# Transposing the FFN input rows once per pair of tiles, before their seven combinations are formed

## The chip, the cores and the metric

The kernel runs on one core of a Trainium2 chip. The core has five engines with instruction queues of their own: PE (TensorE, matmuls and transposes, results in PSUM), DVE (VectorE), ACT (ScalarE), POOL (GpSimd) and SP (SyncE, here only a queue that issues transfers). POOL issues transfers too. The metric is the device time of one execution in microseconds.

## What is computed

One layer of a streaming encoder, in float32, for 2048 prompt rows and 128 sample rows of width 1024: a mixer (attention over a band of chunks beside a convolution), attention into 256 memory tokens, and a SwiGLU feed-forward layer of width 2816. What matters here is the last part of the reference:

```python
h = rmsnorm(x, g_mem_pre)
x = x + rmsnorm(memory_attention(h, mk, mv, w_mq, w_mo), g_mem_post)
h = rmsnorm(x, g_ffn_pre)
f = (jax.nn.silu(h @ w_gate) * (h @ w_up)) @ w_down
x = x + rmsnorm(f, g_ffn_post)
```

## The kernel before

**Stages.** The stages follow one another: memory keys, input projection, attention, mixer output, cross attention (`phase_cross`), gate and up (`gate_up`), down (`down`). The tile framework orders the instructions of each engine ahead of time by a model of their durations, with program order as priority; each engine then runs its queue in that order and waits on semaphores where a producer isn't ready.

**Arithmetic.** A float32 matrix product is made of three products of a rounded half and a rest: each operand is split into `hi` (a cast on ACT) and `lo` (value minus `hi`, mostly on DVE), and PE computes hi x hi, hi x lo and lo x hi (`mm3`, L281 to L283, and `mm3h`, L289).

**Cross stage.** It goes over 16 prompt tiles of 128 rows. For tile t the program has `probs(t)` (eight transposes of the softmax result, L1281, split by L1284 and L1285), `scores(t+1)` (48 matmuls, then the softmax), `norm(t+2)` (load of x1, square and multiply, eight transposes at L316, split) and `values(t)` (48 matmuls, then `postnorm`: square, multiply at L337, the residual added on POOL at L338, store of x2 at L339). The transposes of `probs` and `norm` use one PSUM buffer, tag "t". The load of `norm` needs an "xt" buffer that an earlier `postnorm` has finished with. The sample tile (number 16) is handled earlier, beside other work.

**Fast multiplication of the FFN.** Gate and up are computed with seven block products in place of eight (a Strassen scheme): one half of the blocks is the two 512-wide halves of the input rows of two tiles, the other is weight blocks. So the two tiles of a pair, xa and xb, give seven combinations of their halves. There are three groups of three pairs (`PAIRS`; the last pair is the two halves of the sample tile, 64 rows each), and group g is processed for all 22 hidden chunks of 128 before the next one.

**`natural(g, p)`** (L1298) makes the combinations for one pair: for each tile it loads x2 (L1306, SP), squares it (L1309, ACT), makes the reciprocal root (L1311, L1312, POOL) and multiplies by it and the gain (L1313, DVE). Then POOL forms the four differences (L1314, L1316, L1318, L1320) and stores the seven blocks in rows by 512 columns to `hn[g]` in DRAM, four stores (L1315, L1317, L1319, L1321). Its three buffers "na", "nb" and "nt" exist once. It is called in the cross stage after tile t, from t = 4 on, for the first pair whose tiles are both earlier than t; the pair that remains is called in the first chunks of gate and up (L1484).

**`tform(g, j)`** (L1382) brings combination j of a group into SBUF as `hi` and `lo` with the model dimension on partitions, as PE needs it. For each of the three pairs: load 512 columns of the rows from `hn` (L1388, SP, three buffers "nat"), four transposes (L1391) into a PSUM buffer (two, tag "tr"), cast out of PSUM (L1393, ACT), subtraction out of PSUM (L1394, DVE). A group has 7 x 3 = 21 such blocks. The calls stand: for group 0 before the first chunk, with raised priority, and for each next group during the last chunk of the group before it, form j right after product j has released its buffer (`after(j)`). These two stretches are called turns.

**A chunk** (one f) has seven products of 12 matmuls; the first ends with a copy out of PSUM on ACT (L1450). Beside it run `wforms` for the next chunk (two loads, four POOL operations L1408 to L1411, seven casts L1413, seven subtractions L1414), the activation on DVE (L1469, L1476, L1478 from SBUF, the others from PSUM), and after each second chunk four POOL operations (`act_forms`, L1503 to L1506).

## Time and profile before

| What | Value |
|---|---|
| median of 3 runs | 3066.88 us (3065.92 to 3074.45) |
| span of the profiled execution | 3068.5 us (its own total is not given) |
| mean granted clock of PE | 0.980 |
| cross stage, tiles 0 to 15 | about 1281 to 1644 us of the span |
| gate and up | about 1644 to 2600 us |
| transposes of `tform` (L1391) | 252, in 63 sets of four |
| products of a chunk, groups 0 and 1 | 14.56 us per chunk in steady work |
| products of a chunk, group 2 (320 columns) | 12.32 us per chunk |

In the rows of the profile, a group of instructions is named by its line, engine and operation, with output and input tiles, shape and count; then the busy time in microseconds, the mean duration of one in ns, and the idle time of the engine just before it with what ended it. A mean duration of a matmul is its latency; back to back they overlap, so what one costs PE is read from the distance of the starts, or from the chain of work that ended last. Tiles in SBUF are named sbf, sbr, sbx and flexb, PSUM is psb.

### The profile page before, as it was taken

The numbers are of one execution on the slowest core, as the hardware profiler recorded it, in microseconds if no ns is written. First come the engines' busy times: TensorE is split into PE (matmuls) and PEld (weight loads), VectorE is DVE, ScalarE is ACT, GpSimd is POOL, SyncE is SP. The second block draws the span as 40 slices with busy tenths as digits, with TensorE's granted clock in tenths as the row PEclk, the third lists the DMA queues.
The fourth block names the chain that finished last, engine by engine and source line by source line (L and its number), as shares of the span: only waits on it lengthen the run. The fifth ranks groups of instructions, "written<-read, shape, count | busy, mean of one in ns | idle before, by whom it ended". The sixth has DMA issues, their size and how long they took to land.

```text
span 3068.5 us, 46049 instructions
## 1 busy us (share of the span) xinstructions
PE 2958.1 (96%) x16924; PEld 2725.9 (89%) x16924; DVE 2135.7 (70%) x3077; ACT 1358.3 (44%) x2718; POOL 1419.9 (46%) x1336
## 2 busy tenths in 40 slices
PE   8999999968999999999999999999999999999998
PEld 8999999957888788788888999999999999888786
DVE  6696886746668456635456888877878999556565
ACT  4544455546767344423234333443334444433432
POOL 0267595621112324325355655555555776524413
PEclk9999999978999999999999999999999999999999
DMA  8635252645663456423246333454425345756664
GB/s 302 246 111 176 90 172 97 189 150 135 155 158 141 147 205 209 168 69 124 91 157 206 132 135 135 149 176 159 154 105 174 144 144 178 261 186 210 217 202 161
DMA packets 217693, 500.17 MB, mean 163 GB/s; under 512 B 40757, under 2 KB 104765, under 8 KB 208627
## 3 DMA queue, kind: packets, MB, share of 16 engines
q1 hardware_dynamic: 181035, 427.53, 41.6%
q0 software_dynamic: 36432, 69.70, 7.3%
q8 instruction: 133, 2.18, 0.3%
q14 instruction: 93, 0.76, 0.1%
HBM read 365.97 MB, written 141.81 MB: 165 GB/s over the span
## 4 chain that ended last, share of the span: by engine, by line
PE 38%; DMA 4%; DVE 3%; issue 2%; POOL 2%; ACT 1%; SPq 0%; DVEq 0%; POOLq 0%; ACTq 0%
PE psb L283 12%; PE psb L282 12%; PE psb L281 12%; DMA sbf<-in_w_down_dram 2%; PE psb L289 1%; POOL sbf L1536 1%; DMA sbf<-x 1%; PE psb L1391 1%; DMA sbf<-hn 0%; DVE sbr L1597 0%; DVE sbr L1540 0%; DVE sbr L1414 0%; POOL sbf L338 0%; DMA sbf<-in_w_gate_dram 0%; DVE flexb L1476 0%
## 5 line engine op out<-in xcount | busy, mean ns | idle before, releaser
L281 PE MATMUL psb<-sbr 128*128 128x384 f32 (+3 forms) x2808 | 945.6, 338 | 11.1 <-DVE sbf L688 7.1
L282 PE MATMUL psb<-sbr 128*128 128x384 f32 (+3 forms) x2356 | 808.5, 343 | 2.6 <-DVE sbr L318 2.4
L283 PE MATMUL psb<-sbr 128*128 128x512 f32 (+3 forms) x1848 | 633.4, 344 | 2.7 <-DVE sbr L1597 2.5
L281 PEld LDWEIGHTS psb<-sbr 128*128 128x128 f32 x2808 | 533.0, 190 | 41.0 <-DVE sbf L688 7.3
L283 PE MATMUL psb<-sbr,sbx 128*128 128x384 f32 (+2 forms) x1484 | 478.5, 323 | 0.0
L282 PEld LDWEIGHTS psb<-sbr 128*128 128x128 f32 x2356 | 448.1, 190 | 29.3 <-DVE sbr L318 2.7
L283 PEld LDWEIGHTS psb<-sbr 128*128 128x128 f32 x1848 | 348.6, 189 | 31.6 <-DVE sbr L1597 4.9
L289 PE MATMUL psb<-sbr 128*128 128x512 f32 x1200 | 295.5, 394 | 3.0 <-DVE flexb L1044 1.7
L1414 DVE TENSOR_TENSOR sbr<-sbf,sbr 128x512 fp32r<-128x512 f32 x258 | 263.5, 1024 | 40.7 <-ACT sbr L1413 40.0
L1413 ACT CAST sbr<-sbf 128x512 fp32r<-128x512 f32 x258 | 159.3, 620 | 280.5 <-PE psb L282 232.3
L283 PEld LDWEIGHTS psb<-sbr,sbx 128*128 128x128 f32 x1484 | 282.7, 191 | 0.1
L522 DVE SCALAR_TENSOR_TENSOR psb<-sbf,psb 128x768 f32<-128x768 f32 (+1 forms) x290 | 264.5, 912 | 6.2
L289 PEld LDWEIGHTS psb<-sbr 128*128 128x128 f32 x1200 | 222.4, 189 | 48.7 <-DVE flexb L1044 2.1
L1597 DVE TENSOR_TENSOR sbr<-sbf,sbr 128x384 fp32r<-128x384 f32 (+1 forms) x231 | 168.4, 752 | 93.7 <-ACT sbr L1596 91.2
L276 POOL TENSOR_TENSOR sbx<-sbf,sbr 128x1024 fp32r<-128x1024 f32 x60 | 150.9, 2517 | 85.8 <-ACT sbr L275 81.2
L1596 ACT CAST sbr<-sbf 128x384 fp32r<-128x384 f32 (+1 forms) x231 | 110.7, 497 | 167.7 <-PE psb L282 150.1
L1536 POOL TENSOR_TENSOR sbf<-sbf 128x512 f32<-128x512 f32 x77 | 105.7, 1377 | 168.3 <-DMA sbf<-in_w_down_dram 166.7
L532 POOL TENSOR_TENSOR flexb<-flexb,flexb 128x128 f32<-128x128 f32 (+1 forms) x180 | 168.5, 936 | 30.9 <-ACT flexb L531 20.3
L281 PE MATMUL psb<-sbr,sbx 128*128 128x384 f32 (+1 forms) x524 | 170.6, 327 | 1.2 <-ACT sbr L1393 0.7
L1413 ACT CAST sbx<-sbf 128x512 fp32r<-128x512 f32 x153 | 94.7, 621 | 161.6 <-PE psb L282 152.7
L1414 DVE TENSOR_TENSOR sbx<-sbf,sbx 128x512 fp32r<-128x512 f32 x153 | 151.5, 992 | 15.7 <-ACT sbx L1413 15.5
L1408 POOL TENSOR_TENSOR sbf<-sbf 128x512 f32<-128x512 f32 x66 | 98.6, 1493 | 107.6 <-DVE sbr L1414 50.8
(339 smaller groups left out, 6294.0 us busy)
## 6 DMA issues: line engine op xcount, KB each, us to landing
af<-flexb SPq DMA_DIRECT2D x33, 1344.0 KB, 5.6
sbf<-in_w_down_dram SPq DMA_DIRECT2D x154, 256.0 KB, 3.9
sbf<-af SPq DMA_DIRECT2D x90, 384.0 KB, 4.0
sbf<-in_w_gate_dram SPq DMA_DIRECT2D x66, 512.0 KB, 3.3
sbf<-in_w_up_dram SPq DMA_DIRECT2D x66, 512.0 KB, 3.5
sbf<-x SPq DMA_DIRECT2D x49, 512.0 KB, 3.9
sbf<-in_w_in_dram SPq DMA_DIRECT2D x48, 512.0 KB, 4.2
sbr<-ks POOLq DMA_DIRECT2D x16, 1024.0 KB, 33.9
```

The lines of the kernel that those rows point to most:

```text
L276: self.lo_engine.tensor_tensor(lo[:, :], wf[:, :], hi[:, :].bitcast(F32), ALU.subtract)
L281: nc.tensor.matmul(ps, lh, rh, start=start, stop=False, **kw)
L282: nc.tensor.matmul(ps, lh, rl, start=False, stop=False, **kw)
L283: nc.tensor.matmul(ps, ll, rh, start=False, stop=stop, **kw)
L289: nc.tensor.matmul(y[o], l, r[:, o * 512:(o + 1) * 512], start=start and x == 0, stop=stop and x == 2)
L522: nc.vector.scalar_tensor_tensor(acc if w < CW - 1 else o, src(w), cwt[:, j, w:w + 1], acc, ALU.mult, ALU.add)
L532: nc.gpsimd.tensor_tensor(o, o, v, ALU.add)
L1413: nc.scalar.copy(hs[j][:, :], src[j])
L1414: nc.vector.tensor_tensor(ls[j][:, :], src[j], hs[j][:, :].bitcast(F32), ALU.subtract)
L1536: nc.gpsimd.tensor_tensor(acc[:, :], acc[:, :], q[:, :], ALU.add if s > 0 else ALU.subtract)
L1596: nc.scalar.copy(ch[:, m], a[:, x, m])
L1597: nc.vector.tensor_tensor(cl[:, m], a[:, x, m], ch[:, m].bitcast(F32), ALU.subtract)
```

## The change

`hn[g]` becomes [form, pair position, partition, columns]: the blocks are kept transposed, 128 of the model dimension on partitions and 4 x n columns (four blocks of n rows; n is 128, for the sample pair 64).

`natural` becomes a generator. Each tile is loaded into the buffer "nt" (now `c`), normalised there, transposed in two sets of four on PE, and copied by ACT into "na" or "nb". The four differences are formed by POOL from the transposed tiles, with "nt" taking two of them, and stored. The generator stops after the normalisation of each tile, so that it is advanced at three places. In the cross stage: right after `values(t)` (load and normalisation of the first tile), before the fifth of the eight steps of the next `scores` (transposes of the first tile, load and normalisation of the second), and before the seventh step of the next `values` (transposes of the second, differences and stores). It is started only for t below 14, so two pairs, (2,0) and (2,1), remain for gate and up, where one of its parts is run after each of the first chunks, with the PSUM buffers "tr". In the cross stage it uses the PSUM buffer "t".

`tform` loads a block and splits it straight from SBUF: no transposes, no PSUM. The subtraction for the third pair goes to POOL.

```diff
-        self.hn = [self.dram(f"hn{g}", [P, 3, 7, 512]) for g in range(3)]
+        self.hn = [self.dram(f"hn{g}", [3, 7, P, 512]) for g in range(3)]
...
+            for k in range(KC):
+                if k == 4:
+                    next(side, None)
                 self.mm3h(halves(s), hh[:, k, :], hl[:, k, :], f1[k][0], f1[k][1], k == 0, k == KC - 1)
...
+                if k == 6:
+                    next(side, None)
                 self.mm3h(halves(y), ph[:, k, :], pl[:, k, :], f2[k][0], f2[k][1], k == 0, k == KC - 1)
...
-        def natural(g, p):
+        def natural(g, p, ps, tag):
             n = PAIRS[g][p][2]
+            xa, xb, c = [self.t(pool, [P, D], F32, tg) for tg in ("na", "nb", "nt")]
             for x, (t, r0) in zip((xa, xb), PAIRS[g][p][:2]):
+                nc.sync.dma_start(c[:n, :], self.x2[t][r0:r0 + n, :])
...
+                nc.vector.scalar_tensor_tensor(c[:n, :], c[:n, :], r[:n, :], gffn[:n, :], ALU.mult, ALU.mult)
+                yield True
+                for k0 in range(0, KC, 4):
+                    if k0 == 0 or tag == "tr":
+                        pt = self.t(ps, [P, KC if tag == "t" else 4, P], F32, tag)
+                    kb = k0 if tag == "t" else 0
+                    for k in range(4):
+                        nc.tensor.transpose(pt[:, kb + k, :n], c[:n, (k0 + k) * P:(k0 + k + 1) * P],
+                                            self.ident[:n, :n])
+                    v = x[:, k0 * n:(k0 + 4) * n].rearrange("p (k q) -> p k q", q=n)
+                    nc.scalar.copy(v, pt[:, kb:kb + 4, :n])
+            dst = self.hn[g][p]
+            h0, h1 = slice(0, 4 * n), slice(4 * n, 8 * n)
+            def put(first, src, count=2):
+                nc.gpsimd.dma_start(dst[first:first + count, :, :4 * n].rearrange("f p c -> p f c"),
+                                    src.rearrange("p (f c) -> p f c", f=count))
+            both = slice(0, 8 * n)
+            nc.gpsimd.tensor_tensor(c[:, h0], xb[:, h0], xa[:, h0], ALU.subtract)
+            put(0, xa[:, both])
+            nc.gpsimd.tensor_tensor(c[:, h1], xb[:, h1], c[:, h0], ALU.subtract)
+            put(4, c[:, both])
+            nc.gpsimd.tensor_tensor(xb[:, h0], xb[:, h1], xb[:, h0], ALU.subtract)
+            put(2, xb[:, both])
+            nc.gpsimd.tensor_tensor(xa[:, h1], c[:, h1], xa[:, h1], ALU.subtract)
+            put(6, xa[:, h1], 1)
...
-                if ready and t >= 4:
-                    natural(g, p)
+                if ready and 4 <= t < NPT - 2:
+                    side = natural(g, p, ps_t, "t")
+                    next(side)
...
-                nc.sync.dma_start(x[:n, :], self.hn[g][:n, p, TFORM[j], :])
-                ps = self.t(ps_tr, [P, 4, P], F32, "tr")
-                for k in range(4):
-                    nc.tensor.transpose(ps[:, k, :n], x[:n, k * P:(k + 1) * P], self.ident[:n, :n])
+                nc.sync.dma_start(x[:, :4 * n], self.hn[g][p, TFORM[j], :, :4 * n])
+                x = x[:, :4 * n].rearrange("p (k q) -> p k q", q=n)
                 c = slice(p * P, p * P + n)
-                nc.scalar.copy(hi[:, :, c], ps[:, :, :n])
-                nc.vector.tensor_tensor(lo[:, :, c], ps[:, :, :n], hi[:, :, c].bitcast(F32), ALU.subtract)
+                nc.scalar.copy(hi[:, :, c], x)
+                engine = nc.gpsimd if p == 2 else nc.vector
+                engine.tensor_tensor(lo[:, :, c], x, hi[:, :, c].bitcast(F32), ALU.subtract)
...
-                    if g == 0 and x == 1 and self.todo:
-                        self.natural(*self.todo.pop(0))
+                    if g == 0:
+                        if next(side, None) is None and self.todo:
+                            side = self.natural(*self.todo.pop(0), ps_tr, "tr")
+                            next(side)
```

More of the change, by code (lines that the diff above doesn't have):

```diff
@@ L1258, in norm @@
             return xt, hh, hl
+        side = iter(())
         def scores(hh, hl, where="s"):
@@ L1296, in phase_cross @@
         gffn = self.gain(Region().at("gffn", 4, (self.gffn, [0])), "g_ffn_pre", "gffn")
[L1298 removed]
+        def natural(g, p, ps, tag):
             n = PAIRS[g][p][2]
[L1300 to L1303 removed]
+            xa, xb, c = [self.t(pool, [P, D], F32, tg) for tg in ("na", "nb", "nt")]
             for x, (t, r0) in zip((xa, xb), PAIRS[g][p][:2]):
[L1305 to L1306 removed]
+                nc.sync.dma_start(c[:n, :], self.x2[t][r0:r0 + n, :])
                 junk = self.t(pool, [P, D], BF16, "junk", 1)
                 ss = self.t(pool, [P, 1], F32, "ss", 6)
[L1309 removed]
+                nc.scalar.activation(junk[:n, :], c[:n, :], AF.Square, accum_out=ss[:n, :])
                 r = self.t(pool, [P, 1], F32, "rstd", 6)
@@ L1422, in product @@
                          skip_group_check=True)
+        side = iter(())
         with self.tc.high_priority(offset=HP):
```

16 lines of the change are left out of this document (removed).

## The prediction

> **What bounds the kernel now.** I read the page first (totals, chain), then the stretches around the two stages that the change touches, then single rows.
>
> ```profile
> span 3068.5 us, 46049 instructions
> PE 2958.1 (96%) x16924; PEld 2725.9 (89%) x16924; DVE 2135.7 (70%) x3077; ACT 1358.3 (44%) x2718; POOL 1419.9 (46%) x1336
> PE 38%; DMA 4%; DVE 3%; issue 2%; POOL 2%; ACT 1%; SPq 0%; DVEq 0%; POOLq 0%; ACTq 0%
> ```
>
> TensorE (PE) is busy 96% of the span and is by far the largest owner of the chain. So an instruction taken from PE is time won, unless PE was waiting where it stood anyway. Busy time by stretch (columns: length; then PE, weight loads, DVE, ACT, POOL busy with counts; granted clock; DMA) shows where it waits:
>
> ```profile
> 1380.00:1405.00 25.00, 25.00 (x120) 20.85 (x120) 10.45 (x13) 8.32 (x18) 9.25 (x13) 1.00 0.19 68
> 1645.00:1690.00 45.00, 39.93 (x225) 36.82 (x224) 36.65 (x45) 23.30 (x45) 33.71 (x32) 0.92 0.73 251
> 2003.00:2032.00 29.00, 26.52 (x165) 25.50 (x165) 19.20 (x32) 11.68 (x21) 7.89 (x7) 1.00 0.54 181
> ```
>
> The cross stage (first row) is full, and its other engines are half idle: there PE alone sets the pace. The start of the gate-and-up stage (second row) loses 5.1 us of 45, runs at a clock of 0.92, and DVE and POOL are nearly as busy as PE. The turn from token group 0 to 1 (third row) loses 2.5 us.
>
> **What the transposes cost on PE.** The chain, in order of time, gives a set of four (L1391) and one of eight (L1281) between back-to-back matmuls; the group row gives the count and the waits in front:
>
> ```profile
> 2000.70 0.44 PE psb L1391 x4
> 1608.16 0.87 PE psb L1281 x8
> L1391 PE MATMUL psb<-ident,sbf 128*128 128x128 f32 (+1 forms) x252 | 37.5, 270 | 5.2 <-DMA sbf<-hn 3.3 <-DVE sbr L1394 1.8
> ```
>
> Removed: 63 sets of four, 63 x 0.44 = 27.7 us. Added: 18 tiles of eight. The new rule (t below 14, both tiles earlier than t) starts pairs after t = 4, 5, 6, 7, 10, 11, 12, so 14 tiles lie in the cross stage, 14 x 0.87 = 12.2 us, all of it paid since PE is full there. The other four (pairs (2,0) and (2,1)) go into the first hidden chunks of gate-and-up, 8 sets x 0.44 = 3.5 us. Net on PE 27.7 - 15.7 = 12 us less. But where the 27.7 us stood decides. The copy of the first product out of PSUM (L1450) runs once for each of the 22 hidden chunks of a group and dates them:
>
> ```profile
> 1648.21 0.48 ACT L1450 COPY sbf<-psb 128x384 f32<-128x384 f32 x1
> 1737.35 0.47 ACT L1450 COPY sbf<-psb 128x384 f32<-128x384 f32 x1
> 1955.75 0.48 ACT L1450 COPY sbf<-psb 128x384 f32<-128x384 f32 x1
> 1970.31 0.47 ACT L1450 COPY sbf<-psb 128x384 f32<-128x384 f32 x1
> 2070.82 0.47 ACT L1450 COPY sbf<-psb 128x384 f32<-128x384 f32 x1
> 2303.78 0.47 ACT L1450 COPY sbf<-psb 128x384 f32<-128x384 f32 x1
> 2390.72 0.42 ACT L1450 COPY sbf<-psb 128x320 f32<-128x320 f32 x1
> 2403.04 0.42 ACT L1450 COPY sbf<-psb 128x320 f32<-128x320 f32 x1
> ```
>
> A steady chunk takes 1970.31 - 1955.75 = 14.56 us, in group 2 (320 columns) 2403.04 - 2390.72 = 12.32. *Start*: five chunks take 89.1, 16.3 more than 5 x 14.56; 15 sets of transposes are 6.6 of it, the rest is waits and slow clock. *Turn 1*: six chunks take 100.5, 13.1 over; 21 sets are 9.2, the rest waits. *Turn 2*: 86.9 against 14.56 + 5 x 12.32 = 76.2, 10.8 over, nearly all transposes. The six sets ahead of 1648 stand in the full tail of the cross stage: 2.6 us, gone for certain. The slow clock is seen in the spacing of matmuls, 0.32 us at the start against 0.17 later:
>
> ```profile
> 1655.79 0.52 PE L283 MATMUL psb<-sbr 128*128 128x384 f32 x1
> 1656.11 0.52 PE L281 MATMUL psb<-sbr 128*128 128x384 f32 x1
> ...
> 1999.67 0.33 PE L281 MATMUL psb<-sbr 128*128 128x384 f32 x1
> 1999.84 0.33 PE L282 MATMUL psb<-sbr 128*128 128x384 f32 x1
> ```
>
> **What takes over where the transposes go.** The subtraction that makes the low half (L1394) read PSUM; now it reads SBUF, as L1414 does, 42 times on DVE and 21 times (third pair) on POOL. The source rows give ns min/median/max, the timeline shows DVE, then POOL, in steady work:
>
> ```profile
> L1394 DVE TENSOR_TENSOR sbr<-psb,sbr x45: 408/681/693, 1633.0 to 2339.1; 128x512 fp32r<-128x512 f32 x40, 128x256 fp32r<-128x256 f32 x5
> L1414 DVE TENSOR_TENSOR sbr<-sbf,sbr x258: 674/693/1983, 1612.2 to 2584.5; 128x512 fp32r<-128x512 f32 x129
> ```
> ```profile
> 2473.97 1.39 DVE L1414 TENSOR_TENSOR sbr<-sbf,sbr 128x512 fp32r<-128x512 f32 x1
> ...
> 2475.67 1.39 DVE L1414 TENSOR_TENSOR sbr<-sbf,sbr 128x512 fp32r<-128x512 f32 x1
> ```
> ```profile
> 2473.18 1.63 POOL L1409 TENSOR_TENSOR sbf<-sbf 128x512 f32<-128x512 f32 x1
> 2474.77 1.75 POOL L1410 TENSOR_TENSOR sbf<-sbf 128x512 f32<-128x512 f32 x1
> ```
>
> The PSUM reader never exceeds 693 ns; the SBUF reader ends only when POOL's operation has ended, and one of each takes 2475.67 - 2473.97 = 1.70 us together. I split this into 0.5 for DVE and 1.2 for POOL (an estimate). A chunk then needs 7 + 3 such DVE operations (the three on 384 columns, by their width, at 0.38) and 4 + 2 of POOL (the activations' forms, on 384 columns too, at 0.9): 3.5 + 1.1 + 4.8 + 1.8 = 11.2 us of this shared resource. A turn adds 14 x 0.5 + 7 x 1.2 = 15.4. Six chunks with a turn need 6 x 11.2 + 15.4 = 82.6 us. Against PE's own 87.4 at turn 1 this fits. At turn 2 PE would need 76.2, so 82.6 becomes the floor, 4.3 under today's 86.9, unless the forms prepared ahead and later chunks take up part. At the start 5 x 11.2 + 15.4, and two pairs at 2 x 1.1 + 4 x 1.2 = 7 each, make 85.4 against 89.1. (Pair (2,0) leaves the end of the cross stage: its two loads go on SP behind the 21 form loads and the next weight loads, its squares, multiplies, combinations and stores come some 20 us later, still within these five chunks, so the move itself counts nothing; if it fell behind them it would cost the 7 us in steady chunks, where 11.2 of 14.56 leaves 3.4 each.) The Trainium skill has this as a rule (GPSIMD Engine Reference, section 8, Key points): GpSimd shares its SBUF interfaces with VectorE, with contention for DVE instructions that have two SBUF inputs. The trace agrees: 1.39 us beside POOL, 0.69 alone. By that rule turn 2 gains some 4 us, without it 9; it is the second rival below.
>
> So I take: start -4, the 3.5 us of new transposes included (ends 0 and -13), turn 1 -11 (ends -4 and -13: PE is the floor, but part of the 2.5 us wait for loads stays, since each load buffer is now held until the subtraction instead of the transpose), turn 2 -5 (ends -4 and -11, nearer to the shared floor).
>
> **What the cross stage pays beside the 12.2 us.** Per natural: the x2 load, square, two small POOL operations and the DVE multiply are as before; new are four ACT copies (0.56 each by L1393), and the four POOL combinations now wait for them. ACT has room (8.3 of 25). The three paired stores become two runs of 2 KB per partition where one of 4 KB stood; no row shows such an issue on POOL; between nothing and another 0.62 each it hides in POOL's idle time (9.3 of 25 busy); uncovered, it is 18 x 0.62 = 11 us at most.
> ```profile
> L1393 ACT CAST sbr<-psb 128x512 fp32r<-128x512 f32 (+1 forms) x54 | 29.8, 563 | 28.3 <-PE psb L1391 26.9 <-DVE sbr L1394 1.3
> ...
> L1315 POOL DMA_DIRECT2D hn<-sbf x9 | 5.6, 618 | 1.6 <-DVE sbf L1313 1.5
> ```
>
> What waits now, and what is queued behind it: PE for the normalised tile, with the matmuls of scores and values behind; SP's load of the second tile until PE has read the first out of the same buffer, with norm's x1 load behind; POOL's combinations for ACT's copies, with postnorm's add and store behind, whose end frees the buffer for that x1 load. PE already pays for such chains in this stage:
>
> ```profile
> PE psb L316 <- DVE sbf L313: 4.0, 5, 1.6
> ...
> PE psb L316 <- DVE sbr L318: 3.3, 1, 3.3
> ```
>
> Five waits when norm's multiply comes late, 0.8 us on average, 1.6 at most. For 14 new sets the bounds are 0 and 14 x 1.6 = 22; I take a wait of 0.8 at one set in four, 2.8 us.
>
> **Sum**: 12.2 + 2.8 - 2.6 - 4 - 11 - 5 = -7.6 us. All of it is from one execution with a span of 3068.5; its total is not shown, and its span lies 1.6 above the median 3066.88 of the runs. I apply the difference to the median: **3059 us**.
>
> **Rivals.** *All of it is won*: PE's own work is the floor at the start and both turns, and cross gets no new waits: 12.2 - 2.6 - 12.8 (16.3 less 3.5) - 13.1 - 10.8 = -27; with 6 us of waits left, -21, so 3046. For it: DVE and POOL have idle gaps at turn 1 (19.2 and 7.9 busy of 29). Against: the start.
>
> *The subtraction on the shared interface takes the transposes' place*: nothing at the start, 5 at turn 1, 4 at turn 2: 12.2 + 2.8 - 2.6 - 9 = +3.4, so 3070. This is also the case in which the change doesn't do what it says: the PE work goes, the time doesn't.
>
> *Slower: the loop through the one buffer in the cross stage.* Tile one and tile two are both normalised in "nt", which then takes combinations and is stored before the next pair may load:
>
> ```profile
> DMA to landing us min/median/max: 3.1/4.1/4.5
> ...
> L1309 ACT ACTIVATE sbf<-sbf 128x1024 bf16<-128x1024 f32 x16 | 16.9, 1058 | 16.1 <-DMA sbf<-x 16.0
> L1312 POOL TENSOR_TENSOR sbf<-sbf,mhalf 128x1 f32<-128x1 f32 x16 | 8.9, 558 | 0.9
> L1313 DVE SCALAR_TENSOR_TENSOR sbf<-sbf,flexb 128x1024 f32<-128x1024 f32 x16 | 30.8, 1924 | 24.7 <-POOL sbf L1312 24.6
> L1314 POOL TENSOR_TENSOR sbf<-sbf 128x512 f32<-128x512 f32 x8 | 10.6, 1330 | 0.8 <-DVE sbf L1313 0.8
> L1316 POOL TENSOR_TENSOR sbf<-sbf 128x512 f32<-128x512 f32 x8 | 15.9, 1982 | 0.6
> ...
> DMA to landing us min/median/max: 3.3/3.7/4.8
> ```
> ```profile
> 1390.68 1.04 PE L1281 MATMUL psb<-ident,sbf 128*128 128x128 f32 x8
> ...
> 1414.24 1.04 PE L1281 MATMUL psb<-ident,sbf 128*128 128x128 f32 x8
> ```
>
> A tile takes 4.1 + 1.2 + 1.1 + 1.9 + 0.9 = 9.2; two tiles, copies 1.2, two combinations with issues 4.5 and the store 3.7 make 27.8 us. An iteration of cross is 1414.24 - 1390.68 = 23.6, with the new transposes 25.3. Pairs that follow each other (three steps after t = 4, two after t = 10) slip 2.5 us each. PE can run the next scores meanwhile, half of (23.6 - 1.7) = 11 us, against three slips of 7.5: so I hold it hidden. It decides when the loop passes 25.3 + 11/3 = 29 us. If PE pays the five slips (12.5) and 0.8 at all 14 sets (11.2 instead of 2.8): -7.6 + 12.5 + 8.4 = +13, 3080.
>
> **Chances.** Within 0.3% (9.2 us) a measurement of this kernel can't be told from no change. Forecast 0.46 (own range 3053 to 3066; 0.17 of it below 3057.7), all won 0.25, shared interface 0.17 (0.03 of it above 3076.1), loop 0.12. So faster 0.17 + 0.25 = 0.42, slower 0.12 + 0.03 = 0.15, same 0.43. The range 3043 to 3077 leaves out the better end of the second case and most of the loop.
>
> **What would show it.** Right: 14 sets of eight in the cross stage and about 15 us more there; six chunks at turn 1 near 90 us; at turn 2 near 82; the new subtraction with a maximum far above 693 ns. Wrong: waits of PE for the DVE multiply in the cross stage adding to over 10 us (loop), turns at 77 and 88 us (all won), or turns as long as before with PE waiting for the subtraction.

## The result: slower by 3%, two thirds of it in the cross stage

The changed kernel takes 3166.57 us in the median of four runs, the kernel before 3070.66, also of four: a ratio of 1.0305, with a 95% interval of 1.0285 to 1.0325. The prediction was 3059 us with a range up to 3077, so it was wrong in its direction and far outside its range. Line numbers move in the new program: `probs` has its transposes at L1285 and its split at L1288 and L1289, `natural` its load at L1310, square at L1313, multiply at L1317, transposes at L1324, copies on ACT at L1327, stores at L1332; `tform` has its load at L1411, cast at L1414 and subtraction at L1416; the copy of the first product is L1473, the weights' subtraction L1436. In both programs L317 and L318 are the split (cast, subtraction) of `norm`'s tile behind its transposes at L316. The kernels of the experiments have line numbers of their own.

The page of the changed kernel, its totals:

```profile
span 3171.6 us, 45871 instructions
PE 2984.3 (94%) x16816; PEld 2742.5 (86%) x16816; DVE 2114.7 (67%) x3056; ACT 1378.0 (43%) x2754; POOL 1458.5 (46%) x1357
```

PE has fewer instructions than before (16816 against 16924) and is busy for longer (2984.3 against 2958.1 us): it ran slower, and it also waited more. The view by stretches, cut at the same events in both kernels, says where. The columns are start and end, length, busy time (and count) of PE, weight loads, DVE, ACT and POOL, granted clock, DMA. The rows are: the cross stage from its first `probs` to its last; from there to the first chunk; the start (five chunks); turn 1; turn 2. First before, then after:

```profile
1281.65:1628.40 346.75, 341.54 (x1617) 283.35 (x1616) 161.89 (x174) 111.89 (x243) 142.03 (x170) 1.00 0.32 112
1628.40:1648.21 19.81, 19.37 (x106) 16.26 (x104) 7.51 (x10) 8.42 (x15) 5.72 (x9) 1.00 0.48 154
1648.21:1737.35 89.14, 83.39 (x471) 80.37 (x472) 79.37 (x98) 37.56 (x73) 67.21 (x55) 0.96 0.56 201
1970.31:2070.82 100.51, 98.03 (x594) 96.40 (x593) 82.16 (x118) 44.10 (x82) 49.76 (x37) 1.00 0.55 191
2303.78:2390.72 86.94, 86.23 (x583) 83.47 (x582) 75.44 (x117) 42.12 (x83) 49.17 (x42) 1.00 0.46 161
```

```profile
1288.05:1703.99 415.94, 370.74 (x1726) 306.12 (x1725) 142.11 (x176) 128.28 (x274) 142.87 (x170) 0.93 0.28 94
1703.99:1727.22 23.23, 19.23 (x92) 15.82 (x90) 9.71 (x10) 9.93 (x17) 9.38 (x9) 1.00 0.46 149
1727.22:1821.05 93.83, 81.17 (x432) 79.33 (x433) 78.35 (x88) 40.20 (x77) 64.97 (x52) 0.89 0.44 153
2060.86:2166.68 105.82, 95.69 (x506) 93.30 (x505) 88.23 (x110) 44.94 (x82) 62.39 (x45) 0.94 0.52 179
2399.64:2486.99 87.35, 78.82 (x507) 76.18 (x506) 82.64 (x113) 41.49 (x83) 61.07 (x51) 1.00 0.52 175
```

The cross stage is 69.2 us longer. PE's idle time there rose from 5.2 to 45.2 us, and its busy time by 29.2, of which the new transposes (the group L1324) are 17.5; the granted clock fell from 1.00 to 0.93. The three stretches of gate and up lost their transposes (PE's instructions fell from 594 to 506 at turn 1) and gained nothing: +4.7, +5.3, +0.4. Turn 2 shows it most plainly: PE is busy 7.4 us less and the stretch is as long as before. Beside these rows, the sixteen chunks between start and turn 1 take 239.8 us (1821.05 to 2060.86) instead of 233.0, and the lead into the first chunk 3.4 more. That makes 89.8 of the 103.1 us between the two spans (the medians differ by 95.9; the profiled execution of the changed kernel is the slowest of its four). The other 13 lie ahead of the cross stage (6.4) and behind the last chunk (6.8), where the two programs do the same work; a second profile of the kernel before, below, moved by 3.5 and 3.7 us at the same places, and e6 says why these 13 are not put down to the change.

**What PE waits for in the cross stage.** The view of waits of the changed kernel over that stretch (who waited, for whom; total, times, longest):

```profile
PE psb L316 <- DVE sbf L313: 33.4, 5, 9.0
PE psb L289 <- ACT sbr L317: 8.1, 7, 1.3
PE psb L1324 <- DVE sbr L318: 2.5, 2, 1.3
```

The first row was 4.0 us before. It isn't `natural` that PE waits for, but `norm`: the transposes at L316 stand in PE's queue, and the multiply at L313 in front of them is late. There were five such waits, and five pairs in the stage follow directly on another pair. The timeline of one such iteration of the changed kernel shows how, PE first (start, duration, engine, line; in brackets the idle time before and its releaser):

```profile
1430.29 1.03 PE L1285 MATMUL psb<-ident,sbf 128*128 128x128 f32 x8
...
1444.57 1.03 PE L1324 MATMUL psb<-ident,sbf 128*128 128x128 f32 x8
1445.36 3.43 PE L289 MATMUL psb<-flexb,sbr 128*128 128x512 f32 x14
1454.57 1.94 PE L316 MATMUL psb<-ident,sbf 128*128 128x128 f32 x8 [5.78 <-DVE sbf L313]
1457.62 2.07 PE L289 MATMUL psb<-sbr 128*128 128x512 f32 x4 [1.10 <-ACT sbr L317]
1459.49 1.91 PE L1324 MATMUL psb<-ident,sbf 128*128 128x128 f32 x8
```

and the other queues of the same iteration:

```profile
1434.41 11.55 SPq L1310 DMA_DIRECT2D sbf<-x  x2
```
```profile
1439.20 1.06 ACT L1313 ACTIVATE sbf<-sbf 128x1024 bf16<-128x1024 f32 x1 [6.82 <-DMA sbf<-x]
...
1449.04 1.06 ACT L1313 ACTIVATE sbf<-sbf 128x1024 bf16<-128x1024 f32 x1 [2.75 <-DMA sbf<-x]
...
1450.21 1.06 ACT L306 ACTIVATE sbf<-sbf 128x1024 bf16<-128x1024 f32 x1
```
```profile
1453.14 1.28 DVE L313 SCALAR_TENSOR_TENSOR sbf<-sbf 128x1024 f32<-128x1024 f32 x1 [0.72 <-POOL sbf L299]
```

Read upwards from the wait: L313 needs `norm`'s square (L306 at 1450.21), whose load had been issued at 1426.28; the three loads that SP issued in these 25 us landed in 3.3 us in the median. But ACT runs its queue in order, and ahead of that square stands the square of the pair's second tile (L1313 at 1449.04), which waits for a load. That load may start only when PE has read the first tile out of the one buffer (L1324 at 1444.57). And the first tile itself was loaded late, since the buffer had still to be stored for the pair before (the load at 1434.41, with the square waiting 6.82 us for it). So a loop through one buffer reaches, by ACT's queue, a chain that has nothing to do with it.

### The profile page after: what moved, and what is told of

It is laid out like the page before. It is cut to its first block, busy times and chain, and to the rows that moved or that the text cites. A ratio compares the mean times of both kernels' runs of the same rounds, so it can differ in the third digit from the quotient of the medians.

```text
span 3171.6 us, 45871 instructions
## 1 busy us (share of the span) xinstructions
PE 2984.3 (94%) x16816; PEld 2742.5 (86%) x16816; DVE 2114.7 (67%) x3056; ACT 1378.0 (43%) x2754; POOL 1458.5 (46%) x1357
## 5 line engine op out<-in xcount | busy, mean ns | idle before, releaser
L289 PE MATMUL psb<-sbr 128*128 128x512 f32 x1200 | 307.4, 404 | 13.0 <-ACT sbr L317 8.1
L1436 DVE TENSOR_TENSOR sbr<-sbf,sbr 128x512 fp32r<-128x512 f32 x258 | 256.3, 999 | 28.8 <-ACT sbr L1435 24.6
L1561 POOL TENSOR_TENSOR sbf<-sbf 128x512 f32<-128x512 f32 x77 | 107.1, 1397 | 171.6 <-DMA sbf<-in_w_down_dram 169.9
L1436 DVE TENSOR_TENSOR sbx<-sbf,sbx 128x512 fp32r<-128x512 f32 x153 | 143.6, 943 | 6.1 <-ACT sbx L1435 5.4
L275 ACT CAST sbr<-sbf 128x1024 fp32r<-128x1024 f32 x98 | 102.4, 1049 | 101.2 <-PE psb L282 51.5
```

The lines of the kernel that those rows point to most:

```text
L289: nc.tensor.matmul(y[o], l, r[:, o * 512:(o + 1) * 512], start=start and x == 0, stop=stop and x == 2)
L1436: nc.vector.tensor_tensor(ls[j][:, :], src[j], hs[j][:, :].bitcast(F32), ALU.subtract)
L1561: nc.gpsimd.tensor_tensor(acc[:, :], acc[:, :], q[:, :], ALU.add if s > 0 else ALU.subtract)
```

## The experiments

The table sets the stage lengths of all profiles side by side, cut as above. "Half" means the gate-and-up half of the change alone.

| Kernel | cross | start | turn 1 | turn 2 | ratio to before, 95% |
|---|---|---|---|---|---|
| before, first profile | 346.8 | 89.1 | 100.5 | 86.9 | |
| before, second profile | 346.7 | 90.1 | 99.7 | 87.0 | 0.9999 [0.9973, 1.0024] |
| changed | 415.9 | 93.8 | 105.8 | 87.3 | 1.0305 [1.0285, 1.0325] |
| e0 transposes only | 354.0 | 89.8 | 100.4 | 87.0 | 1.0046 [1.0030, 1.0063] |
| e1 cross half alone | 419.0 | 94.3 | 101.2 | 87.3 | 1.0280 [1.0264, 1.0295] |
| e2 half | 353.9 | 99.8 | 102.0 | 88.6 | 1.0092 [1.0076, 1.0108] |
| e7 half, subtraction on DVE alone | 353.6 | 91.4 | 97.6 | 89.0 | 1.0082 [1.0059, 1.0105] |
| e10 half, rows of 4 KB | 347.2 | 93.2 | 101.6 | 88.6 | 1.0047 [1.0029, 1.0065] |
| e9 half, subtraction out of PSUM | 352.3 | 89.6 | 93.7 | 81.3 | 0.9981 [0.9968, 0.9994] |
| e14 half, both | 348.2 | 86.6 | 93.1 | 80.5 | 0.9972 [0.9956, 0.9988] |
| e3 pairs apart | 369.8 | 89.9 | 107.4 | 87.9 | 1.0143 [1.0109, 1.0176] |
| e4 own buffer | 372.6 | 88.4 | 105.4 | 88.3 | 1.0103 [1.0064, 1.0142] |
| e5 both of these | 365.3 | 91.2 | 107.8 | 90.1 | 1.0148 [1.0111, 1.0184] |
| e12 square after norm | 389.1 | 91.2 | 106.1 | 88.2 | 1.0190 [1.0175, 1.0206] |
| e11 mended | 371.8 | 79.9 | 94.9 | 80.8 | 1.0024 [1.0004, 1.0044] |
| e13 mended, start after norm | 365.3 | 85.7 | 93.3 | 80.3 | 1.0000 [0.9986, 1.0015] |

### Which half, and is it the transposes?

**e0: the transposes alone.** The kernel before, plus

```diff
+        def extra():
+            if now[0] in (5, 6, 7, 8, 11, 12, 13):
+                pt = self.t(ps_t, [P, KC, P], F32, "t")
+                for k in range(KC):
+                    nc.tensor.transpose(pt[:, k, :], gpost[:, k * P:(k + 1) * P], self.ident[:, :])
...
+                if k == 4:
+                    extra()
...
+                if k == 6:
+                    extra()
```

> The kernel before, with 14 extra sets of eight transposes (of a constant tile, read by nothing) at the places in the cross stage where the changed kernel has its own: in the scores and in the values of seven iterations, out through the same PSUM place. Theory A (the cross stage loses its 69 us in waits on the chain that feeds those transposes): only the transposes are paid, 14 x 0.87 = 12 us, so 3076 to 3085 against 3067 to 3071. Rival B (the transposes themselves, the order of the PSUM place and the lower clock cost the 69 us): 3115 to 3140.

The ratio gives 14 us. Its stretch of the cross stage:

```profile
1286.05:1640.06 354.01, 352.84 (x1730) 295.54 (x1729) 155.65 (x174) 112.80 (x243) 140.10 (x170) 1.00 0.32 109
```

The stage grew by 7.3 us, less than the 12.2 that PE works on the sets: the wait for `norm`'s multiply (4.0 before) is gone, as PE comes to it later. The rest of the difference lies ahead of the stage and behind gate and up. Nothing reads these sets, so the copies by ACT are not in this price. So 14 sets in the one PSUM place cost 7 us, not 69; rival B falls.

**e1: the cross half alone.** In the changed kernel, `tform` transposes again:

```diff
-                nc.scalar.copy(hi[:, :, c], x)
...
+                for k in range(4):
+                    nc.tensor.transpose(ps[:, k, :n], x[:n, k * P:(k + 1) * P], self.ident[:n, :n])
...
+                nc.scalar.copy(hi[:, :, c], ps[:, :, :n])
+                nc.vector.tensor_tensor(lo[:, :, c], ps[:, :, :n], hi[:, :, c].bitcast(F32), ALU.subtract)
```

> The changed kernel with the transposes of the gate-and-up stage put back (63 sets of four, the subtraction out of PSUM again), fed with the blocks as they lie; the transposes are then one too many and the values are not the reference's. So the cross stage is changed, the gate-and-up stage is as before. Theory A (the cross stage carries the loss, the gate-and-up stage gives back nearly nothing): 75 us over the kernel before, 3140 to 3155. Rival (the gate-and-up half carries 25 us or more of the loss): under 3130.

3154.19 us, 85 over the kernel before: the cross half carries the loss, as theory A had it.

**e2: the gate-and-up half alone.** The kernel before, with the new `tform` and the new order of rows in DRAM, no transposes in `natural`.

> The kernel before, whose input rows are not transposed at all: the gate-and-up stage loads, casts and subtracts as in the changed kernel, the cross stage is as before (with its stores in the new order of rows); the values are not the reference's. So the gate-and-up half alone. Theory A (the transposes are replaced there by waits of PE for the copy and the subtraction, which have the same length): 3065 to 3085, turn 1 at 100 us or more and turn 2 at 85 or more. Rival (its gain is real and was only hidden by what the naturals left undone): 3045 to 3058, turn 1 near 90.

3097.14 us: 28 *slower* than before, worse than either theory. Turns 1 and 2 are as long as with the transposes, as theory A had it; on top, the start takes 10.7 us more and the cross stage, whose arithmetic is untouched, 7.1. The losses of the two halves, 85 and 28, add up to more than the 96 of the whole; the finer stores are in both. Two causes offer themselves, the stores and the subtraction, and e7, e10 and e9 try them.

### What eats the gain of gate and up

**e7: no subtraction on POOL.** `engine = nc.vector` for all three pairs.

> As the gate-and-up half alone, but the third pair's subtraction on DVE too, none on POOL. If POOL's slow, late subtractions make the waits at the turns (PE waits for L1416 on POOL, 8 us in the changed kernel): 5 to 12 us less than the gate-and-up half alone. If the loads into three buffers that are held until the subtraction make them: within 3 us of it. If DVE itself is the limit there: 3 us or more slower.

3092.12 us, 5.0 less than e2, with intervals that overlap: 8.4 less at the start, 4.4 less at turn 1, 0.4 more at turn 2. PE's waits for the subtraction on POOL (4.9 us at turn 1 in e2) became waits for it on DVE (5.5). By the medians this is the lower end of the first case, by the ratios (3 us) the second: inconclusive.

**e10: rows of 4 KB.** In e2, blocks stored as before (and loaded from these rows, with two loads instead of one for a block of the sample pair):

```diff
-        self.hn = [self.dram(f"hn{g}", [3, 7, P, 512]) for g in range(3)]
+        self.hn = [self.dram(f"hn{g}", [P, 3, 7, 512]) for g in range(3)]
...
-            nc.gpsimd.dma_start(dst[p, 0:2, :n, :].rearrange("f p c -> p f c"), xa)
+            nc.gpsimd.dma_start(dst[:n, p, 0:2, :], xa)
```

> The gate-and-up half alone with the blocks in DRAM laid out as in the kernel before (stores of one run of 4 KB per partition instead of two of 2 KB). If the finer stores cost the 7 us that the cross stage lost in the half alone, with none of its arithmetic changed (353.9 against 346.8): 346 to 348 again, the wait of PE for norm's multiply (L313) back at 4 us from 7.3, and the kernel 3085 to 3092. If not: 352 or more.

The cross stage is back at 347.2 us and the wait for L313 at 4.7; the start gains 6.6, and the ratio falls from 1.0092 to 1.0047. The 6.7 us of the cross stage lie ahead of the first load of a block (1619 us in e2), where only the stores differ, so a store of 2 x 2 KB per partition isn't free there. At the start the loads of the blocks differ too, and the 6.6 us belong to both together. Its issue on POOL takes 0.78 us (first row, e2) instead of 0.61 (second, e10):

```profile
L1315 POOL DMA_DIRECT2D hn<-sbf x9: 691/784/812, 1400.2 to 1709.4; - x9
```
```profile
L1315 POOL DMA_DIRECT2D hn<-sbf x9: 612/612/628, 1400.0 to 1701.2; - x9
```

Three such stores per pair put 0.5 us (an estimate from these rows) in front of the next operation on POOL, `postnorm`'s or `norm`'s small ones, where PE already waited for `norm`'s multiply in the kernel before; that this is the way it comes about is argued, not shown. How much of the 6.7 us comes by the issue and how much by the transfer wasn't separated.

**e9: the subtraction out of PSUM.** In e2, one more copy on ACT:

```diff
+                ps = self.t(ps_tr, [P, 4, P], F32, "tr")
+                nc.scalar.copy(ps[:, :, :n], x)
                 nc.scalar.copy(hi[:, :, c], x)
-                engine = nc.gpsimd if p == 2 else nc.vector
-                engine.tensor_tensor(lo[:, :, c], x, hi[:, :, c].bitcast(F32), ALU.subtract)
+                nc.vector.tensor_tensor(lo[:, :, c], ps[:, :, :n], hi[:, :, c].bitcast(F32), ALU.subtract)
```

> The gate-and-up half alone (input rows not transposed, values not the reference's), with one more copy on ACT: the loaded block goes into PSUM too, and all 63 subtractions are made by DVE out of PSUM, as in the kernel before, none with two SBUF inputs and none on POOL. If the shared interface makes the waits of the half alone (3097.14 us; start 99.8, turn 1 102.0, turn 2 88.6): start 85 to 92, turn 1 88 to 94, turn 2 78 to 84, the kernel 3065 to 3080. If the loads, their three buffers or ACT's queue make them: turn 1 at 98 or more and the kernel within 6 us of the half alone.

Turn 1 falls from 102.0 to 93.7 us and turn 2 from 88.6 to 81.3, the start from 99.8 to 89.6, though ACT does 63 copies more. So the subtraction with both inputs in SBUF is the cause. One thing e9 doesn't separate: a load buffer is now free after ACT's copies and no longer held until the subtraction (at turn 1 ACT's casts wait 18.5 us for loads in e2, its copies 6.8 in e9), so part of the gain may come by the buffers that the slow subtraction held. The source rows of the subtraction show it, min/median/max in ns: in the changed kernel, then in e9.

```profile
L1416 DVE TENSOR_TENSOR sbr<-sbf,sbr x30: 677/1215/2102, 1693.1 to 2426.7; 128x512 fp32r<-128x512 f32 x30
L1416 POOL TENSOR_TENSOR sbr<-sbf,sbr x15: 844/1282/1748, 1710.6 to 2432.3; 128x512 fp32r<-128x512 f32 x10, 128x256 fp32r<-128x256 f32 x5
```
```profile
L1394 DVE TENSOR_TENSOR sbr<-psb,sbr x45: 408/683/693, 1641.2 to 2341.8; 128x512 fp32r<-128x512 f32 x40, 128x256 fp32r<-128x256 f32 x5
```

And the 40 us around turn 1 in which the 21 blocks are made, as stretches: before, e2, e9.

```profile
1985.00:2025.00 40.00, 37.52 (x237) 36.10 (x236) 28.77 (x45) 18.45 (x34) 13.73 (x11) 1.00 0.69 231
```
```profile
2003.00:2043.00 40.00, 33.70 (x176) 31.44 (x174) 36.52 (x45) 17.50 (x33) 26.61 (x17) 0.96 0.73 242
```
```profile
2001.00:2041.00 40.00, 35.21 (x197) 33.67 (x196) 31.21 (x54) 26.49 (x50) 14.62 (x12) 1.00 0.68 239
```

In e2 DVE is busy 36.5 of 40 us (the fourth group of numbers) with no more operations than before (45): they are longer, and PE stands still for 6.3 us. In e9 DVE does 54 operations in 31.2 us. The Trainium skill states the rule (SBUF — State Buffer, section Who interferes with whom): a DVE instruction with two SBUF inputs contends with a GpSimd instruction that reads SBUF, and one with at most one SBUF input, outside the 2-port perf modes, does not. Both halves of it agree with the rows above: a median of 1.2 us and more out of SBUF, 0.69 at most out of PSUM.

**e14: both together.**

> The gate-and-up half alone (input rows not transposed, values not the reference's) with rows of 4 KB and the subtraction out of PSUM: what the removal of the 63 sets of transposes is worth when nothing else is paid. If the three terms add up (cross stage as before, turn 1 -7, turn 2 -6, start 0 to -9): the kernel 12 to 20 us faster than before, 0.994 to 0.996. If the start or the loads take it back: within 0.2% of before.

3066.11 us against 3076.24, a ratio of 0.9972. This is what the removal of 63 sets of transposes is worth when the blocks are transposed nowhere else and ACT makes 63 more copies: 8.6 us by the ratio, between 3.7 and 13.5, less than I expected of it. In its profile turn 1 is 7.4 shorter, turn 2 6.4 and the start 2.5; that is more than the ratio gives, and the profiled execution (3060.73) is one of the faster of its twelve.

### What costs the cross stage 69 us

**e3: no pair follows another.** `if ready and 4 <= t < NPT - 2 and t % 2 == 0`.

> The changed kernel, with a pair started only after every second tile of the cross stage (five there, after tiles 4, 6, 8, 10 and 12; the other four in the gate-and-up stage), so that no pair follows another. Theory A (a pair pays within itself: its second tile can't be loaded before PE has read the first, and norm's square stands behind the second tile's square on ACT): each lone pair still costs what the first of a cluster costs now, 9.5 us, less what the next iteration gives back, so the cross stage takes 372 to 395 us (415.9 now, 346.8 before). Rival B (only pairs that follow each other wait, for the store out of the one buffer): only the transposes are paid, 355 to 360 us. Rival C (each transpose costs 5 us wherever it stands): 5/7 of the loss, 396 us.

369.8 us, just under theory A's range and well above rival B's. The details are against A's mechanism: an iteration with a pair takes 33.2 to 35.0 us, but the next one gives back 5, and the wait for L313 doesn't appear at all. What a lone pair pays, 4.6 us, is its transposes and two short waits in the PSUM place behind `norm`, the only waits of any size in the stage:

```profile
PE psb L289 <- ACT sbr L317: 6.5, 5, 1.3
PE psb L1324 <- DVE sbr L318: 6.3, 5, 1.3
```

So the long waits need a pair that follows another: rival B is right about them, and rival C (396 us) falls.

**e4: a buffer for each raw tile.**

```diff
-                .lay(sbF, 34.5, ("gpost", 4, 1), ("z", 4, 2), ("po", 4, 1), ("ss", 0.015625, 6),
+                .lay(sbF, 34.5, ("gpost", 4, 1), ("z", 4, 1), ("nd", 4, 1), ("po", 4, 1), ("ss", 0.015625, 6),
...
+            raw = [c, self.t(pool, [P, D], F32, "nd") if early else c]
...
+            if early:
+                for (t, r0), c in zip(PAIRS[g][p][:2], raw):
+                    ready(t, r0, c)
```

> The changed kernel with a buffer for each raw tile (the fourth 4 KB come from the second buffer of the exponentials), so that both tiles are loaded, squared and multiplied before the first transpose; all else as changed. Theory A: the first pair of a cluster no longer waits inside itself, but a following pair still waits for the store out of the buffer that its first tile uses (19.6 us from the second tile's transposes to the next pair's first ones): the cross stage takes 380 to 400 us, with 23 to 26 us in the iterations of a first pair (33 now) and 33 to 36 in the others. Rival B (the loop is only inside the pair): 358 to 365. Rival D (the buffer isn't it): 410 or more.

372.6 us with all seven pairs in the same clusters; no wait for L313 is left. (The second tile's square no longer waits for PE either, so this changes the order on ACT along with the buffer.) That is between the two ranges: iterations with a pair take 28 to 32 us, not the 33 to 36 of theory A. So the store behind the pair ahead doesn't make the long waits by itself either. Both parts of the loop are needed, the late first tile and the second tile behind it in the same buffer; breaking either gives back 43 us (e4, seven pairs) or 46 (e3, five).

**e12: the same single buffer, another order on ACT.** The second tile's square is issued after `norm`'s, and with it the small operations on POOL and the multiply on DVE that hang on it:

```diff
                 nc.sync.dma_start(c[:n, :], self.x2[t][r0:r0 + n, :])
+                if x is xb and tag == "t":
+                    yield True
...
                 hq[t + 2] = norm(t + 2)
+            next(side, None)
```

> The changed kernel with one move: the square, scale and multiply of a pair's second tile are issued after norm's for the tile ahead (its load stays where it is, in the one buffer). If the loss comes from norm's square standing behind the second tile's on ACT: PE's wait for norm's multiply (L313, 33 us in the cross stage of the changed kernel) falls under 6 us, and the cross stage to 372 to 388 us from 415.9; the kernel 3115 to 3140. If the one buffer itself, or the store out of it, makes the loss whatever the order on ACT: the wait only changes its name (PE for the second tile's multiply) and the stage stays above 400.

The view of waits over the cross stage (here too L1288 and L1289 are the split of `probs`):

```profile
PE psb L289 <- DVE sbr L1289: 8.6, 1, 8.6
PE psb L289 <- ACT sbr L317: 7.2, 5, 2.0
PE psb L289 <- ACT sbr L1288: 5.9, 4, 2.6
...
PE psb L316 <- DVE sbf L313: 0.9, 1, 0.9
```

The wait for L313 goes from 33.4 to 0.9 us, and the stage to 389.1, one us over the range given: the order of the queues was the link by which the loop reached `norm`, and the timeline above shows ACT's as the one that held it. Moving the second tile's normalisation behind `norm`'s, at the same buffers and the same work, gives back 27 of the 69 us. Some of it comes back as waits for the split of `probs`. The longest, 8.6 us, comes at the end of the stage: L1289 stands on DVE behind two of the weights' subtractions (L1439 in this kernel), and one of these took 8.0 us beside a run of POOL operations:

```profile
L1439 DVE TENSOR_TENSOR sbr<-sbf,sbr x258: 676/692/8005, 1643.9 to 2644.6; 128x512 fp32r<-128x512 f32 x129
```

**e5: pairs apart and own buffers.**

> Both: pairs after every second tile only, and a buffer for each raw tile. Theory A (a loop through the one buffer, inside a pair and between pairs, makes the whole loss): the loss is gone but for the transposes, 5 x 1.7 us, and the new order of the stores, 7 us: the cross stage takes 356 to 364 us, and the kernel 3090 to 3110. Rival (part of the loss has another cause, such as the copies on ACT or the order of the PSUM place): 370 or more.

365.3 us, just over theory A's range, so a small rest has another cause: PE waits 5.3 us for L317 and 5.0 for L318 here, the two steps that stand between `norm`'s transposes and the next in the one PSUM place. The kernel as a whole is not faster than e4 (3122 against 3112 us), because four pairs instead of two now fall into gate and up, where the sixteen chunks behind the start take 245.6 us instead of 234.6.

**e6: the kernel before again.**

> The kernel before once more, for a second profile of it. The five profiles since then show 2.7 to 6.8 us more ahead of the cross stage and 4.1 to 7 us more behind the gate-and-up stage, where none of the kernels differ. If that is only the first profile's execution: this one shows them too (cross stage from 1284 or later, 485 us or more behind the gate-and-up stage). If something that all the changed programs share makes those stages longer: 1281.7 and 481 again.

Cross stage from 1285.2, 484.6 us behind the last chunk, against 1281.7 and 480.9 in the first profile: two profiles of one program differ by 3.5 and 3.7 us (of the expectation's two figures the first was reached, the second missed by 0.4). The kernels that carry the whole change scatter further, with e12's cross stage from 1282.1 and e11's from 1299.8, and with 479.4 us (e13) to 487.8 (the changed kernel) behind the last chunk. So a few us at these places say nothing of a change. That is why the stage lengths are compared here, and not the spans.

### Can the change pay?

**e11: three costs taken away** (own buffers, rows of 4 KB, subtraction out of PSUM).

> The changed kernel with three of its costs taken away: a buffer for each raw tile, rows of 4 KB in DRAM as before, and the subtraction out of PSUM after a copy by ACT. The transposes stay on PE in the cross stage. Where each theory holds: cross stage 362 to 370 us, turn 1 88 to 94, turn 2 78 to 84, the kernel 3070 to 3090; so the change mended comes out no faster than the kernel before, since the cross stage costs more than the turns give back. It would be faster (under 3060) only if the stores and the subtraction are worth more than the 7 and 15 us I give them.

3078.05 us, 1.0024 of the kernel before: start and turns are 20.9 us shorter (9.2, 5.6, 6.1), the cross stage 25.0 longer; cross stage and turn 1 end just above the ranges given. Beside e4, which has the same buffers (372.6), the rows of 4 KB and the rest give back only 0.8 us in the cross stage (371.8), not the 6.7 that they were worth in the half alone. The profiled execution is the slowest of its ten, at 3096.45, and its cross stage begins 14.6 us later than in the second profile of the kernel before.

**e13: and each pair started after norm,** the first tile in the buffer that is free first.

```diff
-            values(t, hq.pop(t)[0], *pp)
             for g, p in list(todo):
...
+            values(t, hq.pop(t)[0], *pp)
```

> The mended kernel (a buffer for each raw tile, rows of 4 KB, subtraction out of PSUM) with each pair started after norm instead of after values, half an iteration earlier in the order of the queues, and with the first tile in the buffer that is free first. If the 25 us that are left in its cross stage come from norm standing behind the next pair's loads and squares (norm then runs just ahead of the scores that need it, two waits of 1.3 us per pair): cross stage 354 to 361 us, and the kernel 0.2 to 0.6% faster than before. If they come from the transposes and the one PSUM place: 368 us or more, and the kernel still 0 to 0.4% slower.

The cross stage takes 365.3 us, between the two ranges, and the kernel is where it was before the change, at 1.0000. The wait for L317 is gone and one for L318 is left (L1334 is the new transposes here):

```profile
PE psb L1334 <- DVE sbr L318: 4.8, 3, 2.2
PE psb L289 <- ACT sbr L1288: 1.1, 1, 1.1
PE psb L316 <- ACT sbf L1274: 1.0, 1, 1.0
PE psb L316 <- DVE sbf L313: 0.9, 1, 0.9
```

So the order explains 6.6 of the 25 us. Of the 18.5 that are left, the transposes cost 7.3 by e0; the other 11.2 are PE's waits, 8.9 us where e0 has 1.2, and 3.5 us of busy time above e0's (356.3 against 352.8), whose cause wasn't sought. It is the best of the kernels that carry the whole change, and it doesn't beat the kernel before.

## Why the prediction was wrong

**The step that failed** is the pricing of the loop through the one buffer. The mechanism was named, with its buffer, its five following pairs and its sign; it was made a rival at 0.12 on this sentence: "PE can run the next scores meanwhile, half of (23.6 - 1.7) = 11 us, against three slips of 7.5: so I hold it hidden." Two things in it were wrong.

- *The cover.* PE runs its queue in order. Between the first tile's transposes (1444.57) and those of `norm` stand 14 matmuls, 3.4 us, not 11; and `norm` can't be passed, since its square stands behind the second tile's on ACT. I listed what is queued behind a waiting PE, SP and POOL, but not what is queued behind ACT's square, which waits for a load. e12 moves that square, with the multiply that hangs on it, and the wait is gone.
- *The loop's length.* I had 27.8 us. The part from the second tile's transposes to the next pair's first ones is 19.6 (1425.01 to 1444.57), close to the 18.6 of my rows. But from the first tile to the second it is 14.9 (1444.57 to 1459.49) where I put 9.2, because `norm`'s chain stands between them. The loop is 34.5 us (34.5 to 37.7 from second tile to second tile over the five following pairs) against an iteration of 25.3, so a slip is 9 or more, not 2.5: beyond the 29 us from which, by my own sum, it decides. The sign that I had given for it, waits for the multiply of over 10 us, came with 33.4.

Point by point:

- *New transposes on PE, 12.2 us*: right as work (PE is busy 11.3 us more in e0's stage); 7.3 us of stage time there.
- *Waits in the cross stage, 2.8 us with 22 as the upper bound*: PE's idle time grew by 40. The bound took the longest wait seen before, 1.6 us, as the longest there could be; a row of the old program bounds no wait that the new order makes.
- *2.6 us gone for certain ahead of the first chunk*: not seen. That stretch went from 19.8 to 23.2 us in the changed kernel, and to 19.3 with the half alone.
- *Turn 1 -11, turn 2 -5*: +5.3 and +0.4. I gave DVE and POOL six whole chunks (87 us) to do 82.6 us of shared work, but the 21 blocks have to be made in the 40 us around the change of groups, where DVE is busy 36.5 of 40 (e2). The second rival, that the shared interface takes the transposes' place, is what happened in gate and up. Without it (e14) the turns reach 93.1 and 80.5, near the 90 and 82 that I had given as the sign of being right.
- *Start -4*: +4.7, and -2.5 in e14. In the half alone it is the new order of rows, stores and loads together (6.6 us, e2 to e10), and the subtraction out of SBUF (6.6, e10 to e14).
- *Finer stores, hidden in POOL's idle time at nothing, 11 us uncovered*: 6.7 us in the cross stage of the half alone (e2 to e10), where PE already waited for `norm`'s chain, and hardly any with a buffer for each tile (0.8, e4 to e11). What they cost in the changed kernel itself wasn't tried.
- *The two late pairs "count nothing"*: the sixteen chunks behind the start lost 6.8 us: one wait of 4.3 us described at the end, and 2.5 us of PE's busy time at a clock of 0.99.

What stays open: turn 1 is 105 to 108 us in all kernels with the whole change and the subtraction out of SBUF, 3 to 6 us more than with the half alone (e2); with the subtraction out of PSUM the difference is gone (93.3 and 94.9 against 93.1 and 93.7). Why the two add up so wasn't tried.

## What to carry to other kernels

When work on a side path gets a new dependence on the main engine, go through *every* in-order queue that the side path uses and ask what of the main path stands behind its waiting instruction: PE's waits of 33 us here came by `norm`'s square on ACT, which needed neither the side path's buffer nor its transposes, and putting it first gave back 27. Busy shares don't show this, and the longest wait of the old program doesn't bound it. And price a removed operation by what its place does for the others: the transposes also brought the blocks into PSUM, where DVE could read them without meeting POOL; 28 us of PE's work were worth 9, and the change pays as much elsewhere.

## What was not expected of the hardware

**A DVE operation can lose several turns in a row to POOL.** The usual price beside POOL is 1.2 to 1.5 us instead of 0.69, one turn. In the changed kernel two of the weights' subtractions took over 3.6, against a maximum of 1.98 before. The timeline of DVE, then of POOL, of the changed kernel, where a late pair's combinations meet those of the weights:

```profile
1832.45 3.65 DVE L1436 TENSOR_TENSOR sbr<-sbf,sbr 128x512 fp32r<-128x512 f32 x1
1836.03 0.54 DVE L1484 TENSOR_TENSOR sbf<-sbf,psb 128x384 f32<-128x384 f32 x1
1836.49 3.85 DVE L1436 TENSOR_TENSOR sbr<-sbf,sbr 128x512 fp32r<-128x512 f32 x1
1840.26 0.54 DVE L1487 TENSOR_TENSOR flexb<-sbf,psb 128x384 f32<-128x384 f32 x1
```
```profile
1836.07 1.29 POOL L1431 TENSOR_TENSOR sbf<-sbf 128x512 f32<-128x512 f32 x1
1837.30 1.27 POOL L1432 TENSOR_TENSOR sbf<-sbf 128x512 f32<-128x512 f32 x1
1838.52 1.27 POOL L1433 TENSOR_TENSOR sbf<-sbf 128x512 f32<-128x512 f32 x1
```

The second of them ends 0.5 us after the third POOL operation in a row has ended. L1487, which reads PSUM and takes 0.54 us, stands behind it, and PE waits 4.3 us for that. In e12 one such subtraction took 8.0 us, as shown above, and PE waited 8.6.

**A wait costs PE twice.** Behind the wait of 5.78 us above, four matmuls take 2.07 us, 0.5 each; the 14 ahead of it took 3.43, 0.25 each. The granted clock is 0.86 in that iteration and 0.93 over the stage. In e4, without the long waits, it is 0.99, and PE's busy time there 359.2 instead of 370.7 us for as many instructions (1726): 11.6 us of the 69 are slower work, not waiting. The Trainium skill has a rule for it (TensorE: Matmul & The Clock Gate, Part 1): the clock is halved after an idle window of about 3.4 us and released after as much sustained work. Stretches behind waits show the granted clock (third figure from the end), first in the changed kernel behind the 5.78 us, then at two of the four places in e4 that stand behind two waits of 1.3 us with four matmuls between them:

```profile
1457.62:1462.00 4.38, 4.38 (x14) 3.75 (x15) 1.20 (x1) 1.15 (x2) 2.61 (x3) 0.50 0.50 123
```
```profile
1449.50:1452.00 2.50, 2.43 (x10) 2.34 (x11) 0.01 (x1) 1.01 (x2) 2.18 (x3) 0.50 0.04 13
1481.00:1484.00 3.00, 3.00 (x18) 2.60 (x17) 0.00 (x0) 1.08 (x2) 2.68 (x3) 1.00 0.29 41
```

The trace agrees on the long wait, behind which the clock is halved. It doesn't agree that it takes an idle window of 3.4 us: in e4 two waits of 1.3 us brought the half clock at two of the four places (for some 6 us and some 3) and left it at 1.00 at the other two.
